# Differential queries and keys split behind their rotation; window outputs fetched apart from their normalization and scaled in one pass

## The chip, the cores and the metric

The kernel runs on one core of a Trainium2 chip. A core has five engines with an instruction stream of their own: TensorE (PE, matmuls, with its weight loads shown as PEld), VectorE (DVE), ScalarE (ACT), GpSimd (POOL) and SyncE (SP, which here issues nearly all DMA transfers). Each works through its stream in order and waits on semaphores for the others. The metric is the device time of one launch in microseconds (us), the median of several runs.

## The reference

One encoder layer on a sequence of 1024 tokens plus 16 meta tokens (length 1040), width 1024, all float32:

```python
h = h + 0.5 * swiglu(rmsnorm(h, ffn1_norm), ...)
u = rmsnorm(h, mix_norm)
z = u @ w_in                       # qa, ka, va (differential), qb, kb, vb (window)
qa, ka = apply_rope(qa), apply_rope(ka)
out_a = diff_attention(qa, ka, va, lam, diff_norm)   # 4 heads, 2 components of 64
out_b = rmsnorm(window_attention(apply_rope(qb), apply_rope(kb), vb, sink), win_norm)
h = h + concat([out_a, out_b]) @ w_out
h = h + 0.5 * swiglu(rmsnorm(h, ffn2_norm), ...)
return rmsnorm(h, final_norm)[:, N_META:]

# diff_attention, each head and tile of queries:
s = einsum('bqhcd,bkhcd->bhcqk', qb, k) * scale
p = softmax(s);  a = p[:, :, 0] - lam * p[:, :, 1];  o = a @ v
# then rmsnorm over the head's 128 values
```

Window attention has 8 query heads over 2 key heads, each query block of 128 sees its neighbours and the meta tokens, and its 512 outputs are normalized together by `win_norm`.

## The kernel before

The program has three stages. The first and the last are the feed-forward parts (lines L226 and L577 of the profile), which the change doesn't touch. Between them lies the mixing stage, from about 750 to 1320 us.

Float32 accuracy comes from splits: a value is rounded to a form that TensorE multiplies fast (`hi`, by a cast on ACT), and the rest `lo = src - hi` is kept beside it. The helper `split` does both, with the subtraction on DVE, or on POOL where it is told so (its lines are L117 and L114). A score then is `q` against `kh` plus `q` against `kl`. For scores, the 64 values of a component fill half of the 128 partitions: `qst` holds `hi` of the queries in its upper and `lo` in its lower half, and `kh` holds the keys' `hi` twice.

Projections. `fillers()` is a generator of pieces of work that the window attention takes a piece at a time. It makes the remaining query pair for the windows, then `ka_pair` and `qa_pair` twice each, and then `early_steps()`. A `pair` projects two row groups (`pj`, L167, written to `z` by ACT at L847), rotates them with the cosine and sine tables (`zs` on POOL and `z` on DVE, L851; sum and difference on DVE, L114) and stores them with `put` in four 32-row blocks each (L870) to DRAM, `ka_d` and `qa_d`. The ring of `z` has 3 buffers, that of `zs` 2.

Window attention runs in 16 units (2 key heads by 8 blocks) of 4 query heads. A unit loads and splits its keys (`kx`, L1026 and L1027), scores them (`ws`, L1040), masks and takes the extreme on DVE (`p`, `mx`, L1044), exponentiates on ACT (L1060), scales on POOL (L1068), transposes (`wt`, L1084), splits the transposed tile (`thi`, `tlo`) and multiplies by the values (`wo`, L1095). The result `ow` goes to DRAM as `ow_d` (L1104). The small operations `es` and `rz` (L1057, L1065) work on 128x4 values.

Differential attention. `load_head` fetches, for each of a head's two components, the keys (`kraw`, L756, twice, once for each half of the partitions) and queries (`qraw`, L757, twice), one buffer each, and converts: ACT casts `kh`, POOL subtracts `kl`, ACT casts `qst` (L759), POOL subtracts its lower half (L760). `kh`, `kl` and `qst` have 3 buffers. `early_steps()` loads head 0, lets `LOAD_GAP` pieces of window work pass, and then makes the first `N_EARLY` = 4 steps. The main loop runs over the other 28 steps of 32 (4 heads by 8 query tiles). A step scores two components (`ds`, six matmuls each, L780), takes the extreme on DVE (`dmx`, L784) and the exponential on ACT (`dp`, L786), combines (POOL L793, DVE L794), transposes (`dt`, L805 and L813, copied to `at` by DVE at L808 or ACT at L810 and L814) and multiplies by the values (`do`, L1228). The next head is loaded in the middle of a head. `out_win` multiplies the window output by its part of `w_out` as a filler from step 9 on.

The window output is normalized by `win_norm`, for 512 positions at a time, at steps 4 and 8: one `own` buffer is fetched from `ow_d` (L1171), squared on ACT (`nacc`, `nsq`, L1148 and L1151) and summed, multiplied by the inverse root on POOL (L1174), scaled to `ow_hi` on ACT (L1176) and to `ow_lo` on DVE (L1177), four times.

What sets the order. The program is not run in the order in which it is written: it is scheduled as a list, by simulated times, into one stream for each engine:

```python
with tile.TileContext(nc, schedule_with_timeline_sim=True) as tc:
```

So a change in one place moves instructions in others. A ring of buffers makes the next writer wait until the last reader of the oldest buffer is done.

Of the kernel before, what the change touches and what calls it, by code (L numbers as in the profile page):

```python
# [10 lines left out]
F32 = mybir.dt.float32  # L11
F32R = mybir.dt.float32r
# [6 lines left out]
P = 128  # L19
# [22 lines left out]
LOAD_GAP = 14  # L42
# [9 lines left out]
def layer(  # L52
# [682 lines left out]
    qa_d = dpool.tile([512, SEQ], F32, name="qa_d")  # L735
    ka_d = dpool.tile([512, L], F32, name="ka_d")
# [8 lines left out]
    def load_head(hd):  # L745
        khs, kls, qs = [], [], []
        for c in range(2):
            row = (hd * 2 + c) * 64
            kraw = kp.tile([P, L], F32, tag="kraw", name="kraw", bufs=1)
            qraw = kp.tile([P, SEQ], F32, tag="qraw", name="qraw", bufs=1)  # L750
            kh = kp.tile([P, L], F32R, tag="kh", name="kh")
            kl = kp.tile([P, L], F32R, tag="kl", name="kl")
            q = kp.tile([P, SEQ], F32R, tag="qst", name="qst")
            for half in range(2):
                hs = slice(half * 64, half * 64 + 64)
                nc.sync.dma_start(kraw[hs, :], ka_d[row : row + 64, :])  # L756
                nc.sync.dma_start(qraw[hs, :], qa_d[row : row + 64, :])  # L757
            split(kh, kl, kraw, nc.gpsimd)
            nc.scalar.copy(q, qraw)  # L759
            nc.gpsimd.tensor_tensor(q[64:P, :], qraw[64:P, :], q[64:P, :].bitcast(F32), op=ALU.subtract)  # L760
            khs.append(kh)
            kls.append(kl)
            qs.append(q)
        v = kp.tile([P, NB + 1, P], F32, tag="v", name="v", bufs=2)
        cs = slice(hd * P, (hd + 1) * P)
        nc.sync.dma_start(v[:, :NB, :], va_d[:SEQ, cs].rearrange("(t p) e -> p t e", p=P))
        nc.sync.dma_start(v[:NM, NB, :], va_d[SEQ:L, cs])
        return khs, kls, qs, v
# [53 lines left out]
    with ExitStack() as st:  # L822
# [43 lines left out]
        def pair(wi, dst, chunks, T, scale, eng=None, first=None):  # L866

            def put(h, z):
                for i in range(4):
                    nc.sync.dma_start(dst[i * 64 + h * 32 : i * 64 + h * 32 + 32, :], z[i * 32 : i * 32 + 32, :T])  # L870

# [19 lines left out]
        def ka_pair(p, eng=None):  # L891
            return pair(5 + 2 * p, ka_d[p * 256 : (p + 1) * 256, :], CH_ALL, L, 1.0, eng)

        def qa_pair(p, eng=None):
            return pair(9 + 2 * p, qa_d[p * 256 : (p + 1) * 256, :], CH_REAL, SEQ, -0.125, eng)
# [93 lines left out]
        def early_steps():  # L989
# [4 lines left out]
            for tag, bufs in (("v", 2), ("qst", 3), ("kh", 3), ("kl", 3), ("kraw", 1), ("qraw", 1)):  # L994
                kp.reserve(tag, bufs)
# [139 lines left out]
    with ExitStack() as st:  # L1135
# [31 lines left out]

        def win_norm(c):
            c0, n = CH_REAL[c]
            ow = npool.tile([P, 4, 512], F32, tag="own", name="own")  # L1170
            nc.sync.dma_start(ow, ow_d[:, :, c0 : c0 + n])  # L1171
            r = rsqrt(sums([ow[:, t, :] for t in range(4)], n), n, 512)
            for t in range(4):
                nc.gpsimd.tensor_tensor(ow[:, t, :], ow[:, t, :], r, op=ALU.mult)  # L1174
                hi = ow_hi[:, t, c0 : c0 + n]
                nc.scalar.mul(hi, ow[:, t, :], wgain[:, t : t + 1])  # L1176
                nc.vector.scalar_tensor_tensor(  # L1177
                    ow_lo[:, t, c0 : c0 + n], ow[:, t, :], wgain[:, t : t + 1], hi.bitcast(F32),
                    op0=ALU.mult, op1=ALU.subtract,
                )  # L1180
# [61 lines left out]
        NQ = 4 * NB  # L1242
        for i in range(N_EARLY, NQ + 4):
# [39 lines left out]
            if i in (4, 8):  # L1283
                win_norm(i // 8)
# [172 lines left out]
```

## Time and profile before

| | us |
|---|---|
| median of 3 runs | 2069.38 |
| lowest and highest | 2064.61, 2073.18 |
| the profiled execution, own time | 2065.43 |
| its span | 2063.7 |
| PE busy | 1942.7 (94%) |
| DVE busy | 1281.4 (62%) |
| ACT busy | 880.0 (43%) |
| POOL busy | 950.8 (46%) |

A busy share is an average over the whole span, and the stages have different limits, so the windows of the mixing stage say more than this table. In a timeline row the bracket at the end tells how long the engine was idle before the row, and which operation's end it then waited for. PEclk is the clock that TensorE was granted, as a share of full speed, 2.4 GHz; 0.50 is its lower level, 1.2 GHz.

### The profile page before, as it was taken

The numbers are of one execution on the slowest core, as the hardware profiler recorded it, in microseconds if no ns is written. First come the engines' busy times: TensorE is split into PE (matmuls) and PEld (weight loads), VectorE is DVE, ScalarE is ACT, GpSimd is POOL, SyncE is SP. The second block draws the span as 40 slices with busy tenths as digits, with TensorE's granted clock in tenths as the row PEclk, the third lists the DMA queues.
The fourth block names the chain that finished last, engine by engine and source line by source line (L and its number), as shares of the span: only waits on it lengthen the run. The fifth ranks groups of instructions, "written<-read, shape, count | busy, mean of one in ns | idle before, by whom it ended". The sixth has DMA issues, their size and how long they took to land.

```text
span 2063.7 us, 30320 instructions
## 1 busy us (share of the span) xinstructions
PE 1942.7 (94%) x11484; PEld 1686.3 (82%) x11484; DVE 1281.4 (62%) x1857; ACT 880.0 (43%) x1630; POOL 950.8 (46%) x807
## 2 busy tenths in 40 slices
PE   5999999999999999999787999998999999989998
PEld 4999999998999889888555777676888888867777
DVE  7855555547874670277877777477655545587745
ACT  6433333334442441365766666353333333334433
POOL 0555554545443750666635433004655454454443
PEclk8999999999999999999898999999999999999999
DMA  4232323228522341533613322523323323475222
GB/s 173 99 118 99 119 83 109 88 100 314 169 70 77 127 147 62 132 104 80 152 49 87 98 67 72 179 92 96 123 103 113 107 77 123 147 265 164 62 82 82
DMA packets 104275, 237.82 MB, mean 115 GB/s; under 512 B 14016, under 2 KB 28816, under 8 KB 104128
## 3 DMA queue, kind: packets, MB, share of 16 engines
q1 hardware_dynamic: 92608, 198.20, 30.7%
q0 software_dynamic: 11520, 37.67, 4.7%
q8 instruction: 90, 1.47, 0.3%
q14 instruction: 57, 0.47, 0.1%
HBM read 169.86 MB, written 65.44 MB: 114 GB/s over the span
## 4 chain that ended last, share of the span: by engine, by line
PE 73%; DVE 11%; ACT 5%; DMA 5%; POOL 3%; issue 3%; SPq 1%; DVEq 0%; POOLq 0%; ACTq 0%
PE p L226 39%; PE pA L577 8%; PE pj L167 4%; PE pC L577 4%; PE pv L936 3%; PE do L1228 2%; PE pd L167 2%; PE ds L780 2%; PE po L167 2%; PE pB L577 2%; DVE bl L114 2%; PE do L167 1%; PE wo L1095 1%; ACT dp L786 1%; DMA wdraw<-wd 1%
## 5 line engine op out<-in xcount | busy, mean ns | idle before, releaser
L114 POOL TENSOR_TENSOR s<-ru 128x512 f32<-128x512 f32 x42 | 55.6, 1323 | 258.1 <-DMA ru<-wu 189.5
L226 PE MATMUL p<-b_hi,wal 128*128 128x260 f32 (+1 forms) x528 | 142.2, 324 | 5.1 <-DVE wal L114 5.1
L226 PE MATMUL p<-t_hi,wch 128*128 128x260 f32 (+1 forms) x528 | 140.8, 321 | 6.5 <-DVE u L114 6.5
L226 PE MATMUL p<-b_hi,wah 128*128 128x260 f32 (+1 forms) x528 | 143.6, 326 | 3.4 <-ACT sg L252 1.9
L226 PE MATMUL p<-b_lo,wah 128*128 128x260 f32 (+1 forms) x528 | 143.3, 324 | 3.3 <-DVE b_lo L114 3.3
L226 PE MATMUL p<-t_lo,wch 128*128 128x260 f32 (+1 forms) x528 | 140.6, 320 | 0.0
L226 PE MATMUL p<-t_hi,wcl 128*128 128x260 f32 (+1 forms) x528 | 140.2, 320 | 0.0
L226 PE MATMUL p<-t_lo,wbh 128*128 128x260 f32 (+1 forms) x504 | 135.9, 320 | 0.0
L114 DVE TENSOR_TENSOR u<-p,m 128x520 f32<-128x520 f32 (+1 forms) x88 | 60.9, 691 | 119.7 <-PE p L226 113.0
L226 PE MATMUL p<-t_hi,wbh 128*128 128x260 f32 (+1 forms) x504 | 133.4, 320 | 0.0
L226 PE MATMUL p<-t_hi,wbl 128*128 128x260 f32 (+1 forms) x504 | 133.3, 320 | 0.0
L117 ACT CAST wch<-ru 128x512 fp32r<-128x512 f32 x88 | 54.6, 621 | 153.8 <-PE p L226 80.0
L117 ACT CAST wbh<-s 128x512 fp32r<-128x512 f32 x84 | 52.1, 620 | 157.0 <-PE p L226 140.3
L577 PE MATMUL pA<-bh,wh 128*128 128x260 f32 (+1 forms) x432 | 116.0, 323 | 1.2 <-DVE h L584 1.2
L577 PE MATMUL pA<-bl,wh 128*128 128x260 f32 (+1 forms) x432 | 115.6, 321 | 0.0
L577 PE MATMUL pA<-bh,wl 128*128 128x260 f32 (+1 forms) x432 | 113.0, 322 | 1.6 <-POOL wl L114 1.6
L117 ACT CAST wah<-rg 128x512 fp32r<-128x512 f32 x88 | 53.9, 621 | 133.2 <-PE p L226 103.2
L114 DVE TENSOR_TENSOR bl<-r,bh 128x520 fp32r<-128x520 f32 (+1 forms) x126 | 107.5, 888 | 3.5 <-ACT bh L117 3.0
L584 DVE SCALAR_TENSOR_TENSOR h<-pA,h 128x520 f32<-128x520 f32 (+1 forms) x96 | 66.1, 690 | 65.7 <-PE pA L577 65.6
L117 ACT CAST wh<-s 128x384 fp32r<-128x384 f32 x96 | 49.0, 513 | 130.5 <-PE pA L577 64.4
L114 POOL TENSOR_TENSOR s<-wr 128x384 f32<-128x384 f32 x48 | 56.1, 1170 | 99.9 <-DVE wl L114 93.5
L226 PEld LDWEIGHTS p<-b_hi,wal 128*128 128x128 f32 x528 | 89.1, 192 | 14.0 <-DVE wal L114 6.2
(299 smaller groups left out, 6144.5 us busy)
## 6 DMA issues: line engine op xcount, KB each, us to landing
rg<-wg SPq DMA_DIRECT2D x44, 512.0 KB, 3.7
ru<-wu SPq DMA_DIRECT2D x44, 512.0 KB, 5.3
wr<-wd SPq DMA_DIRECT2D x24, 768.0 KB, 4.3
r<-g_t SPq DMA_DIRECT2D x12, 780.0 KB, 5.8
r<-g_t SPq DMA_DIRECT2D x12, 768.0 KB, 5.3
g_b<-g POOLq DMA_DIRECT2D x27, 260.0 KB, 5.2
r<-g_b SPq DMA_DIRECT2D x9, 780.0 KB, 5.5
g_b<-g POOLq DMA_DIRECT2D x27, 256.0 KB, 5.5
```

Source lines behind the costliest of these rows:

```text
L114: eng.tensor_tensor(out, a, b, op=op)
L117: nc.scalar.copy(hi, src)
L167: nc.tensor.matmul(o, w, x[:, c0 : c0 + n], start=first and i == 0, stop=last and i == 2)
L226: nc.tensor.matmul(o, w_k(ww, k), x[:, k, c0 : c0 + cn], start=first and k == 0 and i == 0, stop=k == hk - 1 and i == 2, skip_group_check= ...
L577: nc.tensor.matmul(o, w_k(ww, k), xx[:, c0 : c0 + cn], start=new and k == 0 and q == 0, stop=k == DNG - 1 and q == 2, skip_group_check=not ...
L584: nc.vector.scalar_tensor_tensor(hs, full, 0.5, hs, op0=ALU.mult, op1=ALU.add)
L780: nc.tensor.matmul(o, qs[c][:, qt * P : (qt + 1) * P], kk[:, c0 : c0 + n], start=i == 0, stop=i == 1)
L786: nc.scalar.activation(p, full, AF.Exp, bias=mx, scale=-1.0, accum_out=z[:, c : c + 1])
L936: nc.tensor.matmul(ps[:m, 192 + c * 320 : 512 + c * 320], u[:, k, sl], w[:, k, c * 320 : (c + 1) * 320], start=k == 0 and i == 0, stop=k = ...
L1095: nc.tensor.matmul(po, vb[:m, vt, kv, :], t[:m, :], start=j == 1 and i == 0, stop=j == nk + 1 and i == 1)
L1228: nc.tensor.matmul(po[:, :256], v[:m, j, :], at[:m, j, :], start=j == 0, stop=j == NB)
```

## The change

Differential queries and keys are split in `put`, right after the rotation. `hi` takes a buffer of the ring `zs`, the rest stays in `z`, and both are stored to DRAM tensors of their own. `load_head` only fetches then: `qst` in a `hi` and a `lo` half, `kh` from the `hi` tensor twice, `kl` from the `lo` tensor twice. The rings of `kraw` and `qraw` are gone, and `kh` and `kl` have 4 buffers. `LOAD_GAP` goes from 14 to 7. In the window's normalization the fetch is separate (`win_load`): the first stands ahead of the main loop, the second behind the first normalization, which stays at step 4; the second normalization goes from step 8 to step 7. Scale and inverse root are applied in one DVE pass, and `split` with POOL makes the two parts.

```diff
-LOAD_GAP = 14
+LOAD_GAP = 7
...
-    qa_d = dpool.tile([512, SEQ], F32, name="qa_d")
-    ka_d = dpool.tile([512, L], F32, name="ka_d")
+    qa_d = [dpool.tile([512, SEQ], F32, name=f"qa_d{x}") for x in ("hi", "lo")]
+    ka_d = [dpool.tile([512, L], F32, name=f"ka_d{x}") for x in ("hi", "lo")]
...
-            row = (hd * 2 + c) * 64
-            kraw = kp.tile([P, L], F32, tag="kraw", name="kraw", bufs=1)
-            qraw = kp.tile([P, SEQ], F32, tag="qraw", name="qraw", bufs=1)
+            rows = slice((hd * 2 + c) * 64, (hd * 2 + c + 1) * 64)
+            q = kp.tile([P, SEQ], F32R, tag="qst", name="qst")
             kh = kp.tile([P, L], F32R, tag="kh", name="kh")
             kl = kp.tile([P, L], F32R, tag="kl", name="kl")
-            q = kp.tile([P, SEQ], F32R, tag="qst", name="qst")
             for half in range(2):
                 hs = slice(half * 64, half * 64 + 64)
-                nc.sync.dma_start(kraw[hs, :], ka_d[row : row + 64, :])
-                nc.sync.dma_start(qraw[hs, :], qa_d[row : row + 64, :])
-            split(kh, kl, kraw, nc.gpsimd)
-            nc.scalar.copy(q, qraw)
-            nc.gpsimd.tensor_tensor(q[64:P, :], qraw[64:P, :], q[64:P, :].bitcast(F32), op=ALU.subtract)
+                nc.sync.dma_start(q[hs, :].bitcast(F32), qa_d[half][rows, :])
+                nc.sync.dma_start(kh[hs, :].bitcast(F32), ka_d[0][rows, :])
+            for half in range(2):
+                hs = slice(half * 64, half * 64 + 64)
+                nc.sync.dma_start(kl[hs, :].bitcast(F32), ka_d[1][rows, :])
...
-            def put(h, z):
+            def store(dst, h, z):
                 for i in range(4):
                     nc.sync.dma_start(dst[i * 64 + h * 32 : i * 64 + h * 32 + 32, :], z[i * 32 : i * 32 + 32, :T])
 
+            def put(h, z):
+                if isinstance(dst, list):
+                    hi = z_tile("zs")
+                    split(hi[:, :T].bitcast(F32R), z[:, :T].bitcast(F32R), z[:, :T])
+                    store(dst[0], h, hi)
+                    store(dst[1], h, z)
+                else:
+                    store(dst, h, z)
...
-            for tag, bufs in (("v", 2), ("qst", 3), ("kh", 3), ("kl", 3), ("kraw", 1), ("qraw", 1)):
+            for tag, bufs in (("v", 2), ("qst", 3), ("kh", 4), ("kl", 4)):
...
+        def win_load(c):
+            c0, n = CH_REAL[c]
+            owns[c] = npool.tile([P, 4, 512], F32, tag="own", name="own")
+            nc.sync.dma_start(owns[c], ow_d[:, :, c0 : c0 + n])
+
         def win_norm(c):
             c0, n = CH_REAL[c]
-            ow = npool.tile([P, 4, 512], F32, tag="own", name="own")
-            nc.sync.dma_start(ow, ow_d[:, :, c0 : c0 + n])
+            ow = owns.pop(c)
             r = rsqrt(sums([ow[:, t, :] for t in range(4)], n), n, 512)
             for t in range(4):
-                nc.gpsimd.tensor_tensor(ow[:, t, :], ow[:, t, :], r, op=ALU.mult)
-                hi = ow_hi[:, t, c0 : c0 + n]
-                nc.scalar.mul(hi, ow[:, t, :], wgain[:, t : t + 1])
-                nc.vector.scalar_tensor_tensor(
-                    ow_lo[:, t, c0 : c0 + n], ow[:, t, :], wgain[:, t : t + 1], hi.bitcast(F32),
-                    op0=ALU.mult, op1=ALU.subtract,
-                )
+                o = ow[:, t, :]
+                nc.vector.scalar_tensor_tensor(o, o, wgain[:, t : t + 1], r, op0=ALU.mult, op1=ALU.mult)
+                split(ow_hi[:, t, c0 : c0 + n], ow_lo[:, t, c0 : c0 + n], o, nc.gpsimd)
...
+        win_load(0)
         for i in range(N_EARLY, NQ + 4):
...
-            if i in (4, 8):
-                win_norm(i // 8)
+            if i == N_EARLY:
+                win_norm(0)
+                win_load(1)
+            if i == N_EARLY + 3:
+                win_norm(1)
```

Three places show how the streams move. The first is SP where the first pair of differential keys is stored (`ka_d`, among the key loads `kx` of the window units and a weight load `pwraw` of the projections). Before:

```order
L870 DMA ka_d<-z 32x1040
L1026 DMA kx<-kb_d 64x16
L1027 DMA kx<-kb_d 64x384
L1026 DMA kx<-kb_d 64x16
L1027 DMA kx<-kb_d 64x384
L870 DMA ka_d<-z 32x1040 x7
```

Now, on SP at the same place:

```order
L868 DMA ka_dhi<-zs 32x1040 x4
L868 DMA ka_dlo<-z 32x1040 x4
L868 DMA ka_dhi<-zs 32x1040 x4
L868 DMA ka_dlo<-z 32x1040 x4
L1033 DMA kx<-kb_d 64x16
L1034 DMA kx<-kb_d 64x384
```

Sixteen stores stand in a row where eight stood, and the key loads that stood among them come behind.

The second place is SP where head 0 is loaded. Before, the first component's four transfers come first, and a window store and the values `v` behind them:

```order
L756 DMA kraw<-ka_d 64x1040
L757 DMA qraw<-qa_d 64x1024
L756 DMA kraw<-ka_d 64x1040
L757 DMA qraw<-qa_d 64x1024
L1104 DMA ow_d<-ow 256x1x128
L766 DMA v<-va_d 128x8x128
```

Now, on SP at the same place, with the next window store at its end:

```order
L754 DMA qst<-qa_dhi 64x1024
L755 DMA kh<-ka_dhi 64x1040
L754 DMA qst<-qa_dlo 64x1024
L755 DMA kh<-ka_dhi 64x1040
L758 DMA kl<-ka_dlo 64x1040 x2
L754 DMA qst<-qa_dhi 64x1024
L755 DMA kh<-ka_dhi 64x1040
L754 DMA qst<-qa_dlo 64x1024
L755 DMA kh<-ka_dhi 64x1040
L758 DMA kl<-ka_dlo 64x1040 x2
L1111 DMA ow_d<-ow 256x1x128
```

Both components stand together, six transfers each; before, the second stood 17 rows behind the first.

The third place is the second local tile. ACT before, from the first tile's last `ow_hi` (L1176) to the second tile's squares (`nacc<-own`); `dp` are the exponentials of a score:

```order
L1176 ACTIVATE ow_hi<-own,wgain 128x512
L814 COPY at<-dt 16x128
L786 ACTIVATE dp_13220,dz<-ds,dmx_13218 128x1040
L1201 COPY nv<-do 128x512
L810 COPY at<-dt 128x4x128
L1148 ACTIVATE nacc<-own 128x512
```

ACT now, between the same two operations:

```order
L117 CAST ow_hi<-own 128x512
L812 COPY at<-dt 16x128
L784 ACTIVATE dp_13348,dz<-ds,dmx_13346 128x1040
L784 ACTIVATE dp_13275,dz<-ds,dmx_13273 128x1040
L808 COPY at<-dt 128x4x128
L812 COPY at<-dt 16x128
L784 ACTIVATE dp_13401,dz<-ds,dmx_13399 128x1040
L784 ACTIVATE dp_13359,dz<-ds,dmx_13357 128x1040
L1155 ACTIVATE nacc<-own 128x512
```

Four exponentials, of two steps, stand between the two where one stood. And SP now, between the first `own` fetch (two rows above these) and the second:

```order
L755 DMA kh<-ka_dhi 64x1040
L754 DMA qst<-qa_dhi 64x1024
L754 DMA qst<-qa_dlo 64x1024
L755 DMA kh<-ka_dhi 64x1040
L758 DMA kl<-ka_dlo 64x1040 x2
L755 DMA kh<-ka_dhi 64x1040
L754 DMA qst<-qa_dhi 64x1024
L754 DMA qst<-qa_dlo 64x1024
L755 DMA kh<-ka_dhi 64x1040
L758 DMA kl<-ka_dlo 64x1040 x2
L1180 DMA own<-ow_d 128x4x512
```

Before, the second fetch stood three rows behind the first, with one store and one `kraw` load between them; twelve loads stand there now.

## Rows read from the trace of the kernel before

**Rows 1.** Windows by stage: from:to, length, busy us of five engines, PEclk, DMA share, GB/s.

```profile
866.00:980.00 114.00, 112.72 (x611) 92.84 (x610) 78.20 (x155) 65.34 (x158) 79.94 (x65) 1.00 0.37 97
980.00:1061.00 81.00, 62.78 (x307) 44.48 (x306) 66.27 (x125) 56.31 (x124) 42.98 (x44) 0.89 0.48 114
1061.00:1100.00 39.00, 29.40 (x145) 21.90 (x143) 27.75 (x28) 24.77 (x43) 18.75 (x14) 0.96 0.15 45
1100.00:1167.00 67.00, 57.09 (x275) 43.82 (x276) 47.15 (x56) 47.82 (x81) 32.00 (x21) 0.92 0.30 86
1167.00:1226.00 59.00, 55.11 (x299) 44.59 (x298) 43.56 (x51) 39.14 (x70) 26.37 (x17) 1.00 0.35 95
```

**Rows 2.** Timeline, PE: start, us, operation, idle time before it and its releaser.

```profile
988.81 0.46 PE L1040 MATMUL ws<-kxh,wqs 128*128 128x400 f32 x1 [2.07 <-DVE mx L1044]
...
992.69 1.09 PE L1084 MATMUL wt<-ident,p 128*128 128x128 f32 x4 [3.24 <-DVE tlo L114]
994.24 1.02 PE L780 MATMUL ds<-kh,qst 128*128 128x264 f32 x2 [0.47 <-POOL qst L760]
...
1017.06 0.79 PE L1095 MATMUL wo<-thi,vb 16*128 16x512 f32 x1 [2.79 <-DVE ow L1103]
```

**Rows 3.** Timeline, SP, ACT and POOL, the first head's load.

```profile
979.79 1.76 SPq L756 DMA_DIRECT2D kraw<-ka_d  x1
...
987.22 1.06 ACT L117 CAST kh<-kraw 128x1040 fp32r<-128x1040 f32 x1 [1.67 <-DMA kraw<-ka_d]
...
988.36 2.44 POOL L114 TENSOR_TENSOR kl<-kraw,kh 128x1040 fp32r<-128x1040 f32 x1 [2.91 <-ACT kh L117]
990.87 3.32 POOL L760 TENSOR_TENSOR qst<-qraw,qst 64x1024 fp32r<-64x1024 f32 x1
```

**Rows 4.** Tiles qst, kh (1061 to 1167), zs: operation, ns minimum/median/maximum, first and last start.

```profile
L760 POOL TENSOR_TENSOR qst<-qraw,qst x8: 2366/2382/3317, 990.9 to 1223.0; 64x1024 fp32r<-64x1024 f32 x8
...
L117 ACT CAST kh<-kraw x3: 1052/1052/1058, 1088.6 to 1160.9; 128x1040 fp32r<-128x1040 f32 x3
...
L114 DVE TENSOR_TENSOR z<-z,zs x13: 1203/1212/3425, 759.0 to 990.7; 128x1024 f32<-128x1024 f32 x8, 128x1040 f32<-128x1040 f32 x5
```

**Rows 5.** Timeline, DVE at 988.67, and tile rz over the whole span.

```profile
988.67 2.14 DVE L1065 TENSOR_TENSOR rz<-z,es 128x4 f32<-128x4 f32 x1
...
L1065 DVE TENSOR_TENSOR rz<-z,es x16: 141/340/2269, 879.9 to 1039.0; 128x4 f32<-128x4 f32 x16
```

**Rows 6.** Timeline, DVE, SP, ACT and PE, the second local tile.

```profile
1095.95 1.40 DVE L1177 SCALAR_TENSOR_TENSOR ow_lo<-own,wgain,ow_hi 128x512 fp32r<-128x512 f32 x2
...
1097.38 0.58 SPq L1171 DMA_DIRECT2D own<-ow_d  x1
...
1103.16 0.63 ACT L1148 ACTIVATE nacc<-own 128x512 f32<-128x512 f32 x1 [8.12 <-DMA own<-ow_d]
...
1091.74 0.28 PE L813 MATMUL dt<-ident,dp 128*16 128x128 f32 x1 [2.66 <-ACT at L810]
...
1103.10 0.38 PE L813 MATMUL dt<-ident,dp 128*16 128x128 f32 x1 [4.62 <-DVE at L808]
```

**Rows 7.** Windows of 6 us, columns as in rows 1.

```profile
992.00:998.00 6.00, 4.84 (x13) 3.21 (x14) 5.68 (x12) 3.51 (x10) 5.92 (x7) 0.50 0.89 221
...
1100.00:1106.00 6.00, 2.90 (x8) 2.37 (x9) 3.04 (x4) 2.76 (x4) 1.61 (x2) 0.57 0.91 261
```

**Rows 8.** Timeline, SP, ACT and PE, the first stores of differential keys.

```profile
887.56 4.59 SPq L870 DMA_DIRECT2D ka_d<-z  x7
...
894.03 0.60 ACT L847 ACTIVATE z<-pj 128x512 f32<-128x512 f32 x1 [1.87 <-DMA ka_d<-z]
...
899.91 0.39 PE L1095 MATMUL wo<-thi,vb 128*128 128x512 f32 x1
```

**Rows 9.** Tile ow_lo, DVE: ns minimum/median/maximum, first and last start.

```profile
L1177 DVE SCALAR_TENSOR_TENSOR ow_lo<-own,wgain,ow_hi x8: 737/746/2869, 1087.9 to 1132.2; 128x512 fp32r<-128x512 f32 x8
```

**Rows 10.** DMA issues, 980 to 1010 us: count, KB each, median us to landing.

```profile
kraw<-ka_d SPq DMA_DIRECT2D x6, 260.0 KB, 4.5
```

More of the change, by code (lines that the diff above doesn't have):

```diff
@@ L891, in ka_pair @@
         def ka_pair(p, eng=None):
-            return pair(5 + 2 * p, ka_d[p * 256 : (p + 1) * 256, :], CH_ALL, L, 1.0, eng)
+            return pair(5 + 2 * p, [d[p * 256 : (p + 1) * 256, :] for d in ka_d], CH_ALL, L, 1.0, eng)
         def qa_pair(p, eng=None):
-            return pair(9 + 2 * p, qa_d[p * 256 : (p + 1) * 256, :], CH_REAL, SEQ, -0.125, eng)
+            return pair(9 + 2 * p, [d[p * 256 : (p + 1) * 256, :] for d in qa_d], CH_REAL, SEQ, -0.125, eng)
         with mk_pool("pj2", space=PSUM) as psum2:
@@ L1166, in rsqrt @@
             return r
+        owns = {}
+        def win_load(c):
+            c0, n = CH_REAL[c]
+            owns[c] = npool.tile([P, 4, 512], F32, tag="own", name="own")
+            nc.sync.dma_start(owns[c], ow_d[:, :, c0 : c0 + n])
         def win_norm(c):
             c0, n = CH_REAL[c]
-            ow = npool.tile([P, 4, 512], F32, tag="own", name="own")
-            nc.sync.dma_start(ow, ow_d[:, :, c0 : c0 + n])
+            ow = owns.pop(c)
             r = rsqrt(sums([ow[:, t, :] for t in range(4)], n), n, 512)
             for t in range(4):
-                nc.gpsimd.tensor_tensor(ow[:, t, :], ow[:, t, :], r, op=ALU.mult)
-                hi = ow_hi[:, t, c0 : c0 + n]
-                nc.scalar.mul(hi, ow[:, t, :], wgain[:, t : t + 1])
-                nc.vector.scalar_tensor_tensor(
-                    ow_lo[:, t, c0 : c0 + n], ow[:, t, :], wgain[:, t : t + 1], hi.bitcast(F32),
-                    op0=ALU.mult, op1=ALU.subtract,
-                )
+                o = ow[:, t, :]
+                nc.vector.scalar_tensor_tensor(o, o, wgain[:, t : t + 1], r, op0=ALU.mult, op1=ALU.mult)
+                split(ow_hi[:, t, c0 : c0 + n], ow_lo[:, t, c0 : c0 + n], o, nc.gpsimd)
         def head_scale(hd, c, o, r):
```

## The prediction

> **What bounds the kernel now.** I read the stretches first. The change touches the program from about 866 us (the differential keys leave the projections) to the end of the 32 attention steps at 1284 us, and the windows by stage [rows 1] show four regimes there. From 866 to 980 us TensorE (PE) is busy 112.72 of 114 us at full clock: what the other engines do there is covered. From 980 to 1061 us, where the last window units run beside the first differential scores, no engine is full: PE 62.78 of 81 us, VectorE (DVE) 66.27, ScalarE (ACT) 56.31, with a granted clock of 0.89. From 1061 to 1167 us PE works with gaps and a clock of 0.96 and 0.92. From 1167 us on it runs 55.11 of 59 us at clock 1.00; that stretch is eight steps, so 7.4 us is the pace of an undisturbed step. The four steps from 1061 us take 39 instead of 29.5 and the next eight 67 instead of 59: 9.5 + 8 = 17.5 us is what 1061 to 1167 can give back at most.
>
> Next I read PE's gaps in order of time [rows 2], then what leads to them. At 988.81, 992.69 and 994.24 PE idles 2.07, 3.24 and 0.47 us, 5.78 together, and at 1017.06 another 2.79. The chain to the first `ds` [rows 3]: SP issues the keys at 979.79, ACT's cast of them waits for the transfer and starts at 987.22, and GpSimd (POOL) ends its second subtraction at 990.87 + 3.32 = 994.19, where `ds` starts. The gap at 992.69 is named for DVE's `tlo`, and DVE is late because of a 128x4 addition, `rz`, of 2.14 us [rows 5], whose shortest is 0.141. It ran from 988.67 to 990.81, and POOL's subtraction of the keys from 988.36 to 990.80 [rows 3].
>
> In the main loop the second local tile is the late one [rows 6]. DVE ends its `ow_lo` at 1097.35, only then is the one `own` buffer free, SP issues the fetch at 1097.38, and ACT stands 8.12 us in front of `nacc`. Behind ACT wait the copies of the transposed probabilities, and PE idles 4.62 us at 1103.10. It idles 2.66 at 1091.74, behind ACT too. The granted clock falls after both troughs [rows 7]: 0.50 in 992 to 998 us, 0.57 in 1100 to 1106.
>
> **The change, part by part.** *Conversion in the head load.* Removed: per component a cast of keys and one of queries on ACT (1.05 us each [rows 4]) and two subtractions on POOL (2.44 [rows 3] and 2.38 [rows 4]), for eight components 16.8 us of ACT and 38.6 of POOL. Of the chain above, cast to end of POOL is 994.19 − 987.22 = 6.97 us. In exchange each component now loads six 64-row blocks instead of four. Four blocks of some 258 KB took from 981.55 (end of the first issue) to about 987.2 [rows 3, 10]; at the 221 GB/s of 992 to 998 us [rows 7] two more, 0.52 MB, are 2.3 us. So the first `ds` could come 6.97 − 2.3 = 4.7 us sooner. PE also reaches it sooner, since eight window-score matmuls, not 18, stand between the last projection and the first `ds`: less work covers the load. I count 5 of the 5.78 us. Of the 2.79 at 1017.06, 2, since no POOL subtraction runs there any more but window work stays DVE-heavy. Of the 81 × 0.11 = 8.9 us that the lower clock costs in this stretch, 2, as the clock follows the idle time only in part. Two of the eight new splits fall in this stretch and load DVE with 2 × 1.21 = 2.4 us, of which I charge 1. Sum for 980 to 1061: 5 + 2 + 2 − 1 = **8 us gained**. Bounds: 2 (only the end of POOL's chain, with DVE as late as now) and 15 (5.78 + 2.79 = 8.6 us of the gaps, all of them, and 6.4 of the clock).
>
> *Scaling and fetch of the local tile.* Work by engine stays as it was: DVE gets the product (two SBUF inputs; 0.746 us is the median of the nearest row, `ow_lo` [rows 9]) in place of the `ow_lo` subtraction, POOL a subtraction in place of the product, ACT a cast in place of a scaled copy. What moves is the fetch: the first stands ahead of the loop, the second behind the first normalization, and the second normalization's squares stand after four more exponentials (two steps, 2 × 7.4 = 14.8 us) than after the first's last `ow_hi`, instead of after one. The price is SP: twelve loads for later heads now stand between the two fetches and wait for buffers that the last scores of head 0 free. From fetch to landing is some 5.4 us; with the loads ahead of it I expect ACT to wait 1 to 2 us, not 8.12. Taken: 3 of 4.62; 1.7 of 2.66, since three casts of keys and three of queries leave ACT in 1061 to 1167 [rows 4], two of them just ahead of the copy that PE waits for at 1091.74; 0.8 for the other four; and of the clock's 67 × 0.08 = 5.4 us 2.5. Sum for 1061 to 1167: **8 us gained**, between 2 (only the two casts ahead of that copy, 2 × 1.05) and the cap of 17.5.
>
> *Split behind the rotation.* Added: eight casts on ACT, eight DVE subtractions of 1.21 us [rows 4], 32 stores. Six of them, 7.3 us of DVE, lie ahead of 980 us, where DVE is busy 78.20 of 114 us under a full PE: free while that cover holds. The stores are not free. SP takes 4.59 us for seven, 0.65 each, and ACT's `z` at 894.03 already waits 1.87 us for the last of them to leave the buffer [rows 8]. Eight more, queued on the same queue ahead of that release, are 8 × 0.65 = 5.2 us later. Behind the waiting ACT stand the casts of `thi`, for which PE's `wo` waits. PE has projections to do meanwhile and idles 1.28 us in this stretch now, so I charge a share of the 5.2 and no more: **3.5 us lost**, between 0 (PE's projections cover it, as they do now) and 3 × 5.2 = 15.6 (at three later hand-overs of buffers the same, all uncovered).
>
> *LOAD_GAP and more kh, kl buffers* only shift what is issued when; their effect is in the first item.
>
> Net 8 + 8 − 3.5 = 12.5 us. The profiled execution took 2065.43 us, and 2065.43 − 12.5 = 2052.9. The runs shown have a median of 2069.38, 3.95 above it; 2052.9 + 3.95 = **2057 us**.
>
> **The rivals.** *A: the waits remain, in another place.* DVE, busiest in 980 to 1061, sets that stretch, and the second `own` fetch still comes late behind the twelve loads. Then the removed casts and POOL work were off the path: 2 + 5 − 3 = 4 gained, 2065 us. For it: PE's gaps there carry DVE's name. Against it: DVE is at 82%, and part of its time is being held while POOL works.
>
> *B, slower: the stores.* If ACT's wait is paid in full at each of three hand-overs between pairs, with 0.7 us more for the queue that the window's key loads then wait in, 3 × (5.2 + 0.7) = 17.7 us, while only about half of the gains come (8): 9.7 slower, 2079 us. It decides from about 4.7 us of added wait at each, my estimate: 5.9 us lie between ACT's `z` at 894.03 and the `wo` at 899.91 [rows 8], which waits for a cast behind it, less that cast and another of some 0.6. For it: ACT works in order and already waits at 894.03. Against: PE idles 1.28 us in all from 866 to 980 us [rows 1], although ACT's wait is there already.
>
> *C: all stalls go.* Both stretches reach the pace: 15 + 15 − 0 = 30 gained, 2039 us. For it: heads 2 and 3 do run at clock 1.00, and a clock that falls in the troughs gives back more than the trough.
>
> *D: the new DVE passes are held as the old ones were.* The `rz` at 988.67 [rows 5] and an `ow_lo` of 2.869 against 0.746 [rows 9] show DVE held about 2.1 us while POOL worked. Eight new splits and eight products have two SBUF inputs each; half of them held for 2.1 is 17 us of DVE, of which 980 us and later, some ten passes, 10.5 is near the path. With 12.5 − 10.5 = 2 gained, 2067 us. Against: 38.6 us of POOL's work goes at the same time. The Trainium skill, page "SBUF — State Buffer", section "Who interferes with whom", says that a VectorE instruction with two SBUF inputs contends with a GpSimd one that reads SBUF for a shared port pair that is an exclusive lock, so that the later one waits. By that rule the trace agrees: 2.14 against 0.141 us.
>
> **How the numbers follow.** Forecast 52%, C 18%, A 16%, B 9%, D 5%. The forecast's own range is 2050 to 2064 (12.5 give or take half of the two gains). The range wanted reaches a little below C and up past A and D: **2036 to 2072**, which leaves out B and a tail below C, about 13%. Half a percent, 10.3 us, is about what a measurement of this kernel can tell from no change: faster means under 2059. Two thirds of the forecast lie there, 35%, and C: 53%. The rest of the forecast, A and D are the same, 17 + 16 + 5 = 38%. Slower is B, 9%.
>
> **What would show it.** First item: from the last `pj` to the first `ds` some 8 to 10 us, not 14.5 us, no POOL row on `kl` or `qst`, a clock of 0.93 or more from the last projection to the end of the window units, and that stretch 8 us shorter. Second: ACT's wait ahead of the second `nacc<-own` under 2 us, the stretch of head 0's last four steps near 33 us and that of head 1 near 62, with the clock at 0.95 or more. Third: an ACT wait on a `ka_dlo` store of 5 to 8 us near 895 us, with the stretch of the projections 3 to 4 us longer. The prediction is wrong if PE's idle time in that stretch exceeds 6 us, if ACT's wait for `own` stays above 5 us, or if the clock stays at 0.89 although the gaps have gone.

## The result

The changed kernel takes 2085.84 us (median of 5 runs, 2082.30 to 2088.72) against 2070.75 us of the kernel before (5 runs, 2064.61 to 2073.18). The ratio is 1.0078 (95% interval 1.0057 to 1.0098): 15 us slower. Forecast were 2057 us and a range up to 2072; the sign was wrong. The profiled execution has a span of 2086.9 us, 23.2 more than before; some 8 of these are the choice of executions, since the one shown of the kernel before took 2065.43 us (5.3 below its median) and that of the changed kernel 2088.72 (2.9 above).

The same stretches of the changed kernel, bounded where PE has done the same matmul work as at the bounds of [rows 1] (columns: from:to, length, busy us of PE, PEld, DVE, ACT, POOL, PEclk, DMA share, GB/s):

```profile
867.00:985.40 118.40, 114.92 (x612) 94.27 (x611) 79.71 (x160) 71.60 (x162) 91.34 (x69) 0.99 0.47 125
985.40:1067.00 81.60, 65.55 (x310) 46.87 (x309) 64.18 (x129) 53.20 (x123) 24.11 (x34) 0.85 0.56 137
1067.00:1103.00 36.00, 28.77 (x145) 21.25 (x145) 24.95 (x30) 23.59 (x43) 15.51 (x10) 0.95 0.41 106
1103.00:1181.50 78.50, 62.38 (x274) 46.55 (x273) 43.49 (x52) 41.45 (x73) 24.99 (x20) 0.87 0.38 98
1181.50:1242.50 61.00, 55.84 (x297) 44.30 (x295) 43.69 (x51) 36.17 (x66) 15.50 (x12) 1.00 0.23 71
```

Against the 114, 81, 39, 67 and 59 us of before the projections lose 4.4, the stretch of the first scores 0.6 where it was to gain 8, the one from 1067 us gains 3, the one from 1103 us loses 11.5 at a clock of 0.87, and the last loses 2. One gain of 8 us was looked for in the second stretch, the other in the third and fourth together.

The first `ds` does come sooner. PE's timeline, then SP's, ACT's and POOL's at the second local tile, in the order of the engines' rows (start, us, operation, idle time before it and its releaser), all of the changed kernel:

```profile
989.96 0.72 PE L778 MATMUL ds<-kh,qst 128*128 128x264 f32 x3 [2.49 <-DMA kh<-ka_dhi]
...
992.28 1.21 PE L778 MATMUL ds<-kl,qst 128*128 128x264 f32 x3 [1.16 <-DMA kl<-ka_dlo]
...
1008.92 0.70 PE L1047 MATMUL ws<-kxh,wqs 128*128 128x400 f32 x1 [3.79 <-DVE mx L1051]
...
1111.63 1.11 PE L803 MATMUL dt<-ident,dp 128*128 128x128 f32 x4 [3.97 <-ACT at L808]
...
1125.37 1.23 PE L778 MATMUL ds<-kh,qst 128*128 128x264 f32 x3 [3.83 <-ACT dp L784]
...
1100.41 1.24 SPq L758 DMA_DIRECT2D kl<-ka_dlo  x2
1103.46 0.56 SPq L1180 DMA_DIRECT2D own<-ow_d  x1
...
1109.96 0.63 ACT L1155 ACTIVATE nacc<-own 128x512 f32<-128x512 f32 x1 [3.85 <-DMA own<-ow_d]
...
1121.58 0.69 ACT L1166 ACTIVATE nr<-do,eps 128x512 f32<-128x512 f32 x1 [2.19 <-PE do L1161]
...
1097.00 6.43 POOL L114 TENSOR_TENSOR ow_lo<-own,ow_hi 128x512 fp32r<-128x512 f32 x4
```

From the last `pj` (982.46) to the first `ds` it is now 7.5 us where it was 14.5 [rows 2, 3]. But the second `own` fetch is issued at 1103.46, later than the 1097.38 of [rows 6], in the moment in which POOL ends the first tile's four subtractions (1097.00 + 6.43 = 1103.43). It was never fetched ahead: there is one `own` buffer, and its last reader is now POOL. ACT's wait is shorter (3.85 for 8.12) only because more of ACT's work stands ahead of it.

To see where time goes I laid the executions over one another by work: the undisturbed lengths of all matmuls added up in PE's order, and how many us later (+) or sooner a kernel reaches the same sum than the kernel before. It is one execution of each, and executions of one kernel differ by some us; steps of 4 us and more within a row are what to read. The column at 1103 lies at the end of the 4.62 us wait of [rows 6] and can be off by as much.

| at (us of before) | 960 | 980 | 1020 | 1060 | 1103 | 1121 | 1150 | 1290 |
|---|---|---|---|---|---|---|---|---|
| changed kernel | +1.8 | +5.4 | +3.4 | +6.1 | +2.7 | +13.7 | +13.2 | +19.0 |
| first part alone (split_only) | +1.1 | +4.8 | −0.6 | +0.7 | −1.5 | −2.4 | −4.4 | +4.9 |
| second part alone (win_only) | +0.7 | +0.7 | +0.5 | +1.5 | +7.1 | +11.5 | +12.5 | +12.6 |
| second part, fetch ahead (win_two) | +0.3 | +0.3 | −0.2 | +1.1 | +2.7 | +1.5 | −2.1 | −0.8 |
| changed, fetch ahead (after_two) | +2.3 | +5.0 | +0.5 | +4.2 | +5.7 | +0.8 | −2.5 | +4.0 |

Three steps of the changed kernel ask for a cause: +4 near 965 us, +11 between 1103 and 1121, and +6 after 1150.

### The profile page after: what moved, and what is told of

The parts are those of the page before. It is cut to its first block, busy times and chain, and to the rows that moved or that the text cites. A ratio compares the mean times of both kernels' runs of the same rounds, so it can differ in the third digit from the quotient of the medians.

```text
span 2086.9 us, 30339 instructions
## 1 busy us (share of the span) xinstructions
PE 1957.7 (94%) x11484; PEld 1694.7 (81%) x11484; DVE 1270.7 (61%) x1865; ACT 873.5 (42%) x1622; POOL 920.1 (44%) x791
## 4 chain that ended last, share of the span: by engine, by line
PE 71%; DVE 11%; DMA 6%; ACT 4%; POOL 4%; issue 3%; SPq 0%; POOLq 0%; DVEq 0%; ACTq 0%
PE p L226 38%; PE pA L577 8%; PE pC L577 4%; PE pv L943 3%; PE pj L167 3%; PE pd L167 2%; PE do L1237 2%; PE pB L577 2%; PE po L167 2%; PE ds L778 2%; DVE bl L114 2%; PE do L167 1%; DMA wq<-qb_d 1%; POOL wqs L986 1%; PE wo L1102 1%
## 5 line engine op out<-in xcount | busy, mean ns | idle before, releaser
L114 DVE TENSOR_TENSOR wal<-rg,wah 128x512 fp32r<-128x512 f32 x88 | 69.8, 800 | 51.2 <-ACT wah L117 50.5
L226 PEld LDWEIGHTS p<-b_hi,wah 128*128 128x128 f32 x528 | 89.3, 193 | 13.5 <-ACT sg L252 2.5
```

Of the source, the lines that this page charges most:

```text
L114: eng.tensor_tensor(out, a, b, op=op)
L226: nc.tensor.matmul(o, w_k(ww, k), x[:, k, c0 : c0 + cn], start=first and k == 0 and i == 0, stop=k == hk - 1 and i == 2, skip_group_check= ...
```

## The experiments

All ratios are to the kernel before on the same chip, with 95% intervals.

| kernel | median us | before | ratio |
|---|---|---|---|
| split_only | 2072.65 | 2068.07 | 1.0020 (1.0006 to 1.0035) |
| win_only | 2075.14 | 2068.07 | 1.0031 (1.0012 to 1.0049) |
| gap_only | 2068.36 | 2068.07 | 0.9998 (0.9984 to 1.0012) |
| split_win | 2081.48 | 2068.07 | 1.0061 (1.0038 to 1.0085) |
| win_two | 2064.92 | 2070.14 | 0.9979 (0.9966 to 0.9991) |
| win_dve | 2078.90 | 2070.14 | 1.0044 (1.0028 to 1.0060) |
| split_q4 | 2071.53 | 2070.14 | 1.0014 (0.9998 to 1.0029) |
| after_two_q4 | 2076.62 | 2070.14 | 1.0031 (1.0016 to 1.0045) |
| win_step8 | 2076.98 | 2068.57 | 1.0045 (1.0027 to 1.0063) |
| before_two | 2065.21 | 2068.57 | 0.9985 (0.9974 to 0.9996) |
| after_two | 2068.80 | 2068.57 | 1.0003 (0.9990 to 1.0015) |
| split_nosub | 2063.13 | 2068.57 | 0.9975 (0.9964 to 0.9986) |
| split_pool | 2068.72 | 2069.42 | 0.9996 (0.9984 to 1.0009) |
| two_pool | 2072.90 | 2069.42 | 1.0014 (1.0002 to 1.0027) |
| two_pool14 | 2063.59 | 2069.42 | 0.9970 (0.9957 to 0.9983) |
| two_pool14_q4 | 2061.18 | 2066.54 | 0.9971 (0.9959 to 0.9982) |

### The parts

The first part alone is the change's diff without its normalization and with `LOAD_GAP = 14`; the second is the normalization alone; the third is

```diff
-LOAD_GAP = 14
+LOAD_GAP = 7
```

on the kernel before, and split_win is the changed kernel with that line undone.

> The kernel before with the first part of the change alone: queries and keys split behind the rotation, kh and kl with 4 buffers; gap 14, normalization as before. Theory 1 (the six loads per component crowd SP: the second own fetch stands behind twelve of them, and the 16 stores in a row delay window loads): most of the loss is here, 2078 to 2086 us, with an ACT wait of 3 us or more before the second nacc<-own. Theory 2 (the earlier second normalization costs it): about as before or faster, 2060 to 2070. Theory 3 (the shorter gap costs it): 2060 to 2070.

> The kernel before with the second part alone: own fetched ahead, scaled in one DVE pass, second normalization at step 7. Theory 1: as before within 5 us or faster by up to 8, since only one key load stands between the two fetches. Theory 2: 2078 to 2086. Theory 3: 2066 to 2072.

> The kernel before with LOAD_GAP 7 in place of 14, nothing else. Theories 1 and 2: 2066 to 2074, no difference. Theory 3 (early scores push the end of the window units back, and with it both normalizations): 2078 to 2086.

> The changed kernel with LOAD_GAP back at 14. Theory 1: 2080 to 2088, as the changed kernel. Theory 2: the same. Theory 3: 2062 to 2070, the loss is gone.

No theory held by itself: split_only and win_only came out between the ranges that the theories had named. The normalization costs something (1.0031) and so does the split (1.0020; the two intervals overlap), the gap alone nothing, and the first two together 1.0061. Theory 1 was wrong in its main point: twelve loads do stand ahead of the second fetch in split_only, but SP had issued them by then; the fetch went out at 1094.80, in the moment in which DVE ended `ow_lo`, as before.

### The one buffer of the local tile

win_two and after_two let the second fetch land where nothing is needed until head 2, and multiply from there:

```diff
+                raw = o_lo[:, 2:4, :].bitcast(F32)
+                owns[c] = [raw[:, t // 2, t % 2 * 512 : t % 2 * 512 + 512] for t in range(4)]
+                for t in range(4):
+                    nc.sync.dma_start(owns[c][t], ow_d[:, t, c0 : c0 + n])
...
         win_load(0)
+        win_load(1)
...
                 win_norm(0)
-                win_load(1)
```

before_two puts the same fetches into the kernel before and leaves the rest of it. win_dve leaves the one buffer and subtracts on DVE, win_step8 leaves it and normalizes at step 8, both on win_only:

```diff
-                split(ow_hi[:, t, c0 : c0 + n], ow_lo[:, t, c0 : c0 + n], o, nc.gpsimd)
+                split(ow_hi[:, t, c0 : c0 + n], ow_lo[:, t, c0 : c0 + n], o)
```

```diff
-            if i == N_EARLY + 3:
+            if i == N_EARLY + 4:
```

> The second part alone, but with the second fetch really ahead: it lands in a part of the tile o_lo that is idle until head 2, so it needs no buffer that the first normalization has to free. Measured without this: 2075 us against 2068 before, the fetch issued when POOL ended the first tile's last ow_lo at 1102.49 us (before: when DVE ended it, 1097.35). Theory F (the one buffer, now freed by POOL, is the cost): 2062 to 2069 and no ACT wait ahead of the second nacc. Theory P (POOL's subtractions stand among the head load's conversions and delay scores) or theory S (the normalization at step 7): 2072 to 2078.

> The second part alone, with the subtraction for ow_lo on DVE instead of POOL. Theory F: the buffer is free about as early as before, 2066 to 2071. Theory P: 2064 to 2070 too, but with no wait of ds for POOL's qst at the spot where the second part had 1.83 us. Theory S: 2072 to 2078.

> The second part alone, with its second normalization back at step 8; one own buffer. Theory S (at step 7 the waiting instruction stands ahead of work of the steps that could have filled the wait for the one buffer): 2066 to 2071, as before, although the fetch is issued no earlier than 1097 us. Theory F alone (the late fetch is the cost wherever the normalization stands): 2073 to 2078.

> The kernel before with nothing changed but the fetches: both ahead of the loop, the second one into the idle part of o_lo; POOL product, DVE subtraction and step 8 as before. If the 8.12 us that ACT waits for the second tile cost time in the kernel before: 2060 to 2066, as with the second part repaired (2064.9 against 2070.1). If that gain came from scaling on DVE or from step 7: 2067 to 2072.

> The changed kernel with the second fetch ahead, qst at 3 buffers. The changed kernel is 15 us over before (ratio 1.0078), and with both repairs 6.5 (1.0031). Theory F: most of that step is this repair's, 2074 to 2080. If the fourth qst buffer brought it: 2082 to 2088.

The fetch decides. SP issues the second fetch in win_two at 1068.60, 34 us sooner than win_only (timeline, SP, of win_only and then of win_two), and in after_two at 1075.02, 28 us sooner than the changed kernel:

```profile
1102.52 0.56 SPq L1173 DMA_DIRECT2D own<-ow_d  x1
```

```profile
1068.60 1.77 SPq L1179 DMA_DIRECT2D o_lo<-ow_d  x4
```

and the second part goes from 1.0031 to 0.9979, the changed kernel from 1.0078 to 1.0003: 15 us. The third and fourth stretch of after_two, bounded by about the same work (429 matmuls for 419), are 40 and 63.5 us, where the changed kernel has 36 and 78.5 (windows of after_two, columns as above):

```profile
1065.00:1105.00 40.00, 29.82 (x134) 21.73 (x133) 23.27 (x28) 28.99 (x51) 17.41 (x14) 0.87 0.52 138
1105.00:1168.50 63.50, 57.61 (x295) 45.63 (x295) 48.17 (x56) 37.60 (x69) 25.03 (x17) 0.97 0.41 105
```

Together that is 103.5 us for 114.5. Of the clock the changed kernel lost 36 × 0.05 + 78.5 × 0.13 = 12.0 us in them, after_two 40 × 0.13 + 63.5 × 0.03 = 7.1, so by this estimate some 5 of these 11 us are clock and the rest is waiting. Behind each of its two troughs (stretches in which PE idles) the changed kernel works at the lower of the two levels: the granted clock is 1.00 from 1102 to 1108 us and then this (windows, columns as above):

```profile
1114.00:1120.00 6.00, 5.66 (x20) 4.27 (x20) 3.86 (x4) 4.28 (x7) 4.37 (x4) 0.50 0.07 20
...
1126.00:1132.00 6.00, 5.33 (x12) 3.20 (x12) 5.02 (x7) 2.79 (x6) 0.49 (x1) 0.50 0.00 0
```

That is added to the troughs' own length.

Two expectations failed here. after_two came out faster than the 2074 to 2080 us that it was given, and win_dve slower than all of its ranges. win_dve was to be as before, since the buffer is free early again. It is: the fetch goes out at 1097.25 and ACT waits 4.93 us (timelines, SP, ACT and PE, of win_dve).

```profile
1097.25 0.57 SPq L1173 DMA_DIRECT2D own<-ow_d  x1
...
1103.61 0.63 ACT L1148 ACTIVATE nacc<-own 128x512 f32<-128x512 f32 x1 [4.93 <-DMA own<-ow_d]
...
1102.88 0.38 PE L813 MATMUL dt<-ident,dp 128*16 128x128 f32 x1 [5.06 <-DVE at L808]
...
1124.05 0.74 PE L780 MATMUL ds<-kh,qst 128*128 128x264 f32 x3 [4.33 <-ACT dp L786]
```

Yet it takes 2078.9. In the kernel before ACT waits longer at that place and PE about as long [rows 6], and it loses only 3 us by it (before_two, 0.9985). One difference is what PE has in its stream around the wait. In the kernel before it is this (timeline, PE):

```profile
1096.59 1.89 PE L1228 MATMUL do<-at,v 128*128 128x256 f32 x8
...
1103.27 3.62 PE L1228 MATMUL do<-at,v 128*128 128x256 f32 x8
```

Eight products with the values run up to the wait of 4.62 us [rows 6], and eight more stand right behind it. In win_dve none stand there, and a second trough (4.33, the inverse root and its table loads) follows with no cover. win_step8, with the order of the steps restored, lost as much, although sixteen products stand ahead of its wait there, so the cover alone does not explain it. Nor does the hour of the fetch: split_win, at 1.0061 (the split's cost included), issues it as early as the kernel before (timeline, SP, of split_win):

```profile
1097.36 0.56 SPq L1180 DMA_DIRECT2D own<-ow_d  x1
```

What is shown is that each of the three kernels in which the second fetch was put ahead became faster by it (before_two, win_two, after_two). Which property of the order sets the price, between 3 and 15 us, the runs leave open. before_two and win_two are equal within their intervals: scaling in one DVE pass and step 7 bring nothing measurable.

### The subtractions behind the rotation

split_nosub leaves out the eight DVE subtractions, split_pool moves them to POOL:

```diff
-                    split(hi[:, :T].bitcast(F32R), z[:, :T].bitcast(F32R), z[:, :T])
+                    nc.scalar.copy(hi[:, :T].bitcast(F32R), z[:, :T])
```

```diff
-                    split(hi[:, :T].bitcast(F32R), z[:, :T].bitcast(F32R), z[:, :T])
+                    split(hi[:, :T].bitcast(F32R), z[:, :T].bitcast(F32R), z[:, :T], nc.gpsimd)
```

> The first part alone without the eight DVE subtractions after the rotation: the unsplit values are stored as the second part, all stores and loads stay. The first part alone is at 2072.65, and in its trace PE falls 3.9 us behind near 965 us, where POOL's scaling took 6.57 us for four in the changed kernel and its wqs came late. Theory L (DVE's new passes with two inputs hold POOL): that step is gone, 2066 to 2070. Rival (the sixteen stores in a row delay what SP fetches): the step stays, 2071 to 2074.

> The first part alone with its eight new subtractions on POOL (2.4 us each) instead of DVE (1.21). Measured: 2072.65 us on DVE, 2063.13 without them. Theory L (the cost is POOL being held by the DVE passes, PE's 1.93 us wait for wqs at 965 us and the half-rate stretch after it): POOL does the work later but is not held, and the step near 965 us goes or stays under 2 us, 2064 to 2070. Rival (POOL is the late engine there whoever adds to it: 2 x 2.4 us more on POOL ahead of wqs): the step is as large or larger, 2072 to 2079.

Left out, they give back about 9 us (1.0020 − 0.9975), more than was expected and nearly their 8 × 1.21 = 9.7, though six of them lie where PE was full. The step near 965 us is 3.7 of it (split_only in the table, from 960 to 980); where the rest is lost is not shown. The timeline of split_only at that step (DVE, POOL, PE):

```profile
959.32 1.22 DVE L114 TENSOR_TENSOR z<-z,zs 128x1040 fp32r<-128x1040 f32 x1
...
961.67 1.22 DVE L114 TENSOR_TENSOR z<-z,zs 128x1040 fp32r<-128x1040 f32 x1
...
954.72 6.58 POOL L1075 TENSOR_SCALAR p<-p,rz 128x272 f32<-128x272 f32 x4
961.39 3.72 POOL L986 TENSOR_TENSOR wqs<-wq,wqs 64x1024 fp32r<-64x1024 f32 x1
...
965.15 0.39 PE L1047 MATMUL ws<-kxh,wqs 128*128 128x272 f32 x1 [1.93 <-POOL wqs L986]
```

The same POOL rows of split_nosub:

```profile
952.72 4.96 POOL L1075 TENSOR_SCALAR p<-p,rz 128x272 f32<-128x272 f32 x4
957.76 2.40 POOL L986 TENSOR_TENSOR wqs<-wq,wqs 64x1024 fp32r<-64x1024 f32 x1
```

The two subtractions of the second key pair run exactly while POOL scales and splits the window queries, and POOL's rows grow by 1.62 and 1.32 us, 2.94 for the 2.44 that DVE works. POOL is the late engine there: PE waits 1.93 us for `wqs`, and the granted clock is 0.66 from 965.1 to 970 us after 1.00 from 955 to 965. In split_pool POOL does the work itself; its rows have their usual 4.93 and 2.40 us again, PE has no gap over 0.3 us from 955 to 985 us, and the first part is at 0.9996 (timelines of split_pool, POOL and PE).

```profile
954.48 4.93 POOL L1075 TENSOR_SCALAR p<-p,rz 128x272 f32<-128x272 f32 x4
959.38 4.86 POOL L114 TENSOR_TENSOR z<-z,zs 128x1040 fp32r<-128x1040 f32 x2
964.32 2.40 POOL L986 TENSOR_TENSOR wqs<-wq,wqs 64x1024 fp32r<-64x1024 f32 x1
...
969.45 0.37 PE L1047 MATMUL ws<-kxh,wqs 128*128 128x272 f32 x1
```

But `wqs` is no sooner for it: it is done at 966.72, in split_only at 965.11. PE doesn't wait because the score that needs it stands later in this order, at 969.45 instead of 965.15. So that the DVE passes stretch POOL's rows is shown by split_nosub; that split_pool is faster because POOL is not held is not, since its order is another one.

The Trainium skill, page "SBUF — State Buffer", section "Who interferes with whom", says that with a VectorE instruction of two SBUF inputs and a GpSimd one that reads SBUF the later one is blocked, whichever it is. The trace agrees that GpSimd can be the one that loses, 6.58 against 4.96 us; I had thought of the other way round alone. It doesn't agree by the rows' starts: POOL's `wqs` starts at 961.39, 0.28 us ahead of the DVE subtraction, and it is POOL's row that is stretched.

### The query buffers and the gap

split_q4 and after_two_q4 (the latter with the fetch ahead too) give `qst` a fourth buffer, and `nt` shares that of `nsq` to make room:

```diff
-            for tag, bufs in (("v", 2), ("qst", 3), ("kh", 4), ("kl", 4)):
+            for tag, bufs in (("v", 2), ("qst", 4), ("kh", 4), ("kl", 4)):
```

> The first part alone with 4 buffers for qst instead of 3 (nt shares the buffer of nsq to make room). Measured with 3: 2072.65 us, and PE waits 2.54, 2.31 and 1.42 us for the transfer of queries before a head's second component. Theory Q (without a staging tile the queries can only be fetched when a qst buffer is free, so the fetch shows): the three waits are gone and 2064 to 2069. Rival (the longer store queue and DVE's new passes before 980 us are the cost): 2071 to 2075.

> The changed kernel with both repairs: the second fetch lands in the idle part of o_lo, qst has 4 buffers. If theories F and Q hold together, what the change was to bring in the loads is left: 2055 to 2068. If neither holds: 2080 to 2088. If the parts disturb one another by their order (the window units end later with the short gap): 2070 to 2078.

Without a staging tile queries are fetched only when a `qst` buffer is free, and that shows in the first part alone (timeline, PE, split_only):

```profile
1096.12 1.00 PE L778 MATMUL ds<-kh,qst 128*128 128x264 f32 x3 [2.54 <-DMA qst<-qa_dlo]
...
1165.58 0.72 PE L778 MATMUL ds<-kh,qst 128*128 128x264 f32 x3 [2.31 <-DMA qst<-qa_dlo]
```

With four buffers no such wait is left, but the time stays (1.0014 for 1.0020), and PE waits elsewhere. In split_q4 DVE's copy for a transpose now stands behind two reductions of scores that came sooner (timelines, PE and DVE):

```profile
1152.20 0.28 PE L811 MATMUL dt<-ident,dp 128*16 128x128 f32 x1 [2.37 <-DVE at L806]
...
1149.17 2.37 DVE L782 TENSOR_REDUCE dmx<-ds 128x1 f32<-128x1040 f32 x2
1151.47 0.67 DVE L806 COPY at<-dt 128x512 f32<-128x512 f32 x1
```

Both repairs together (after_two_q4, 1.0031) were slower than the fetch alone (after_two, 1.0003); four buffers are not a repair.

So the third step of the changed kernel, after 1150 us, keeps no shown cause. It stands in the table's rows with the split (split_only from −4.4 to +4.9, after_two from −2.5 to +4.0) and in none without (win_only from +12.5 to +12.6).

Last, both working repairs with either gap, and the fourth buffer on the better one:

> The changed kernel with the second fetch ahead and the new subtractions on POOL. The changed kernel with the fetch ahead alone is as before (1.0003). Theory L: 2060 to 2066, faster than both kernels. Rival: 2068 to 2075.

> The same with LOAD_GAP 14 in place of 7. If the gap matters only where the order makes it (alone it changed nothing, 2068.36 against 2068.07): within 4 us of the same kernel with 7. If the short gap costs beside the split, as 2085.84 against 2081.48 hinted: 3 to 5 us faster than with 7.

> The fastest kernel so far (second fetch ahead, new subtractions on POOL, gap 14; ratio 0.9970) with a fourth qst buffer. All kernels with the split fall back by 8 to 11 us in the last three heads, 3.7 of it in waits of ds for transfers of queries. If those waits are the cost: 2058 to 2061 (ratio 0.994 to 0.9955). If PE only waits elsewhere once they are gone, as the first part with four buffers hinted (2071.53 against 2072.65, its waits replaced by waits for DVE's copies): within 2 us of 2063.6.

two_pool14 beats both kernels: 2063.59 us, 0.9970. With the gap of 7 it is 2072.90, where 2060 to 2066 were expected: there the subtractions on POOL bring nothing over after_two. So beside both repairs the gap costs 9 us, though alone it cost nothing; without the repairs it is 1.0078 for 1.0061 (split_win), and those intervals overlap. The fetch ahead with the gap of 14 and the subtractions on DVE was not run. Fetches of the first local tile differ too (timelines, SP, of two_pool and of two_pool14):

```profile
1067.72 0.58 SPq L1181 DMA_DIRECT2D own<-ow_d  x1
```

```profile
1058.70 0.58 SPq L1181 DMA_DIRECT2D own<-ow_d  x1
```

With 7, ten scores of a component stand ahead of the last `wo`, with 14 nine, and the window's output, with what follows from it, comes 9 us later; one score more doesn't account for that. Whether this delay is the cost no run isolates, and gap_only speaks against it: its first fetch goes out at 1063.92, 4 us later than that of the kernel before, and it loses nothing. The fourth buffer adds nothing again (0.9971).

## Why the prediction was wrong

**The step that failed is the second item**, the fetch of the second tile: "the first stands ahead of the loop, the second behind the first normalization" was read as a fetch ahead. I counted what stands between two instructions of ACT and of SP and left out what the fetch itself waits for, the release of the one `own` buffer. The rows had it: [rows 6] show the fetch issued 0.03 us after `ow_lo` ended. In the changed kernel the last read went from DVE (0.75 us each) to POOL (1.6), and the release came 6 us later; but that alone is not the price, since win_dve and split_win, released as early as before, lose too. Expected were 8 us gained; the same part by itself lost 7 (win_only), and the changed kernel with the fetch really ahead is 15 us faster (after_two). Of the 17.5 us that I took as the cap, taking this wait out of the kernel before gave 3.4 (before_two). My sign, ACT's wait, could not tell: 3.85 us lie between the 2 that were to confirm the item and the 5 that were to refute it, and the loss stood in the stretch of head 1, 78.5 us instead of some 62.

**The first item** had the arrival of `ds` right and what it is worth wrong. `ds` comes 7.5 us behind the last `pj` (8 to 10 foretold), but the stretch is 0.6 us longer and not 8 shorter. The terms that failed are the 5 of 5.78 us and 2 of 2.79 us of waits and the 2 us of clock: PE now waits 2.49 us for `kh`, 1.16 for `kl` and 3.79 for DVE's `mx`, 7.4 in place of 8.6, and the clock did not rise from 0.89 but fell to 0.85. That is rival A, the waits remain in another place. By the table the kernels with the split make up 2 to 5 us between 980 and 1020 and give 1 to 4 of it back by 1060.

**The third item** was right in size by luck and wrong in cause. 3.5 us of loss were foretold, the stretch of the projections is 4.4 longer and the step near 965 us 3.7, but not through the stores: at the first hand-over ACT has no wait for a store at all, and in two_pool14, where it waits 3.16 us for `ka_dlo`, PE lost nothing by it. "Free while that cover holds" was the error, a term put at nothing: the cover was PE's, and POOL, whose rows the DVE passes stretch, had none. All eight passes together cost about 9 us (split_nosub). Rival D had the lock and looked at it from DVE's side only. Rival B, the slower side, had a close time and a mechanism that no run shows.

**What I called an effect "in the first item", LOAD_GAP,** was no effect alone and 9 us beside the split and both repairs. A sum over separate edits had no term for it.

**The chances** gave 9% to slower. Rival A did keep the late fetch, behind the twelve loads, and priced it as a gain of 4 us all the same. A forecast whose gain rests on a wait that disappears should have had, as its first rival, that the wait stays and costs more.

## What to carry to other kernels

A fetch is ahead only if its destination is free ahead: look for the buffer's last reader and that engine's queue before counting the instructions between. Moving a pass to an idle engine can hold the engine beside it, so check what the neighbour does in that stretch even where TensorE is full. Here a trough cost its own length and the slower clock behind it, so small waits in a tightly packed order were worth removing, and their removal (another destination for one fetch, 15 us) was worth more than the conversions that the change meant to save.

## What was not expected of the hardware

DVE subtractions of 1.22 us with two SBUF inputs stretched POOL's overlapping rows by 1.6 and 1.3 us, more than DVE's own time in all (2.94 for 2.44).

Of the clock: in the changed kernel two troughs 14 us apart (3.97 us up to 1111.63, 3.83 up to 1125.37) were each followed by a stretch at the lower level, 0.50 from 1114 to 1120 and from 1126 to 1132, and the clock was 1.00 again from 1138 us on. after_two, with one trough of 3.86 us there (up to 1103.51), has 0.70 from 1105 to 1111 us and 1.00 from 1111 on. I had not expected two waits of 4 us to bring the mean over 78.5 us down to 0.87.
